# Attention scores of two heads side by side on half the array's rows each, in a hybrid SSD and attention layer

## The chip, the cores and the metric

The kernel runs on one core of a Trainium2 chip. The metric is device time in microseconds (us) of one execution; lower is better. Engines are named as the profile names them: PE is TensorE's matrix product, PEld its loading of weights (the stationary operand), DVE is VectorE, ACT ScalarE, POOL GpSimd, and SP the engine whose queue issues most DMAs. A q behind a name (SPq) is that engine's sequencer.

## What is computed

One decoder layer over 512 tokens of width 1024, all in float32. A normalised input goes through one wide projection; its columns feed a Mamba-2 scan (16 heads) and, beside it, forgetting attention (FoX, 16 heads of 64). Both results go through one output projection, and a gated MLP follows. The part that the change touches is the attention:

```python
qh = rms_norm(heads(q), q_norm_w)
kh = rms_norm(heads(k), k_norm_w)
log_f = jax.nn.log_sigmoid(f_raw + f_bias)
cum = jnp.cumsum(log_f, axis=1).transpose(0, 2, 1)
for start in range(0, s, Q_BLOCK):          # blocks of 128 queries
    end = start + Q_BLOCK
    logits = jnp.einsum('bhqd,bhkd->bhqk', qh[:, :, start:end], kh[:, :, :end]) * HEAD_DIM ** -0.5
    logits = logits + cum[:, :, start:end, None] - cum[:, :, None, :end]
    p = jax.nn.softmax(jnp.where(causal, logits, -jnp.inf), axis=-1)
    outs.append(jnp.einsum('bhqk,bhkd->bhqd', p, vh[:, :, :end]))
```

## The kernel before

Nearly all products are made in a split form. A float32 matrix is written as a high part h, rounded to the fast format float32r, and a low part l, the rest; a product a x b is then the sum of ah x bh, ah x bl and al x bh, three matmuls into one PSUM bank (`mm3`, L97 to L102, so most matmuls of the profile carry line L100). ACT makes h by a copy, DVE makes l by a subtraction, for each weight tile that SP's queue has loaded (`load_split`, L86).

The program is written as a sequence of stages, and a scheduler interleaves them. Parts inside `urgent()` go ahead of the rest when their inputs are ready, and the rest fills up. `tc.keep_in_program_order` pins an instruction: pinned instructions keep the order in which they are written, and others may still be put between them. What stands on an engine in the end is one fixed order, in which each instruction waits for its own inputs.

Stages: at the start (L194 to L219) the transposed input comes in eight tiles, each scaled by the norm's weights into xh and xl (`split_x`, L169), with dt's small product (L205, L209: 64 and 32 columns of the array) and the first wide product (`first_product`, L184) between. Then come projections and the SSD scan, the attention, the second norm, and the MLP ("up" products, and "X", "Y", "Z" for the down-projection).

The attention (L709 to L722) works on pairs of heads, p = 0 to 7:

- `fox_qk` (L545): PE transposes the pair's k and q (tile qkT, L552). The pair's two heads then stand in rows 0 to 63 and 64 to 127 of a PSUM bank. Each head's half is split by ACT (L559) and DVE (L560). For a head, qs holds qh in one half of the rows and ql in the other; ks[.,0] holds kh in both halves and ks[.,1] holds kl in both. The second copy of k is made by ACT and DVE for pair 0 (L562, L563) and by a DMA between partitions for the others (L567).
- `fox_bias` (L570): the forgetting term and the causal mask of a head, written into its tile prob by ACT and POOL.
- `fox_scores` (L592): for each of the four query blocks, with n = 128, 256, 384, 512 keys, two matmuls over all 128 rows (L600, L601) give (qh + ql) x kh + (qh + ql) x kl in one bank, S. DVE then adds the bias and finds the maximum (L602), ACT makes the exponential (L606), and DVE divides (L610).
- `fox_turn` (L612): PE transposes the probabilities (pT, L623), ACT copies them out (L625).
- `fox_values` (L628): PE multiplies by v (o, L633), in plain float32. The two heads of a pair use columns 64 to 127 and 0 to 63 of the array in turn, all pinned. In plain float32 one product is two matmuls in the profile.

The fillers between these steps are projections of later heads (`project`, banks pw; `project_v`, banks pq) and output projections (banks po), all of `mm3`. Banks qkT, S, pT come from one pool of four PSUM banks (`mbank`); pw, pq, po from another of three.

Of the kernel before, what the change touches and what calls it, by code (L numbers as in the profile page):

```python
# [15 lines left out]
P = 128  # L16
# [18 lines left out]
LOW_PART = {}  # L35
C_MIX, C_SCW, C_SCB, C_FCW, C_FCB, C_QW, C_KW, C_END = 0, 8, 56, 68, 200, 244, 245, 246
# [3 lines left out]
def tile_hybrid_layer(  # L40
# [35 lines left out]
    taken = {}  # L76

    def low_part(key):
        order = LOW_PART.get(key, "d")
        n = taken.get(key, 0)  # L80
        taken[key] = n + 1
        return dve if order[n % len(order)] == "d" else pool

    loads = [0]

    def load_split(src, sub=None, four=True):  # L86
# [7 lines left out]
        (sub or dve).tensor_tensor(out=l, in0=r, in1=raw(h), op=ALU.subtract)  # L94
        return h, l
# [73 lines left out]
    def split_x(k, xr):  # L169
        w = pc[:, C_MIX + k : C_MIX + k + 1]  # L170
        act.activation(xh[:, k, :], xr, AF.Copy, scale=w)
# [24 lines left out]
    load_dt()  # L196
    for k in range(NK):
        xr = load_x(k)
        if k == 0:
            nc.sync.dma_start(pc[:, 0:NK], pcol[:, 0:NK])  # L200
        split_x(k, xr)
        if k in (1, 3):
            split_first(*load_first(k // 2))
# [15 lines left out]
    nc.sync.dma_start(pc[:, NK:], pcol[:, NK:])  # L219
# [6 lines left out]
    def feature_tile(src, o=None):  # L226
        h, l = src if isinstance(src, tuple) else load_split(src, sub=low_part("feat"))
# [8 lines left out]
    second, third = [load_split(wxbc[j], sub=dve) for j in (10, 0)]  # L236
# [11 lines left out]
    def out_proj(pairs, m, halves=(0, 1)):  # L248
        for half in halves:
            ws = [load_split(wout[pair, half], sub=low_part("o%d" % pairs[0])) for pair in pairs]  # L250
# [80 lines left out]
    def token_block(src, key="tb"):  # L331
        tiles = [bank("pq") for _ in range(2)]
        for kh in range(2):
            h, l = load_split(src[kh], sub=low_part(key))
# [12 lines left out]

    def wide_block(src, key, use, behind=None):
        ws = []
        for b in range(2):  # L350
            tiles = [bank("pw") for _ in range(2)]
            for kq in range(4):
                if b == 0:
                    ws.append(load_split(src[kq], sub=low_part(key)))
# [190 lines left out]
    def fox_qk(pair, tq, tk):  # L545
        qs = [pf.tile([P, SEQ], F32R, tag="qs", name="qs", bufs=4) for _ in range(2)]
        ks = [pf.tile([P, 2, SEQ], F32R, tag="ks", name="ks", bufs=4) for _ in range(2)]
        pr = pair % 2
        for tok, w in ((tk, kw), (tq, qw8)):
# [3 lines left out]
            for hd, (own, other) in enumerate(HALVES):  # L553
                src, sw = t[own, :], w[own]
                if tok is tq:
                    h, l = qs[hd][own, :], qs[hd][other, :]
                else:
                    h, l = ks[hd][own, 0, :], ks[hd][own, 1, :]
                act.activation(h, src, AF.Copy, scale=sw)  # L559
                dve.scalar_tensor_tensor(out=l, in0=src, scalar=sw, in1=raw(h), op0=ALU.mult, op1=ALU.subtract)  # L560
                if tok is tk and pair == 0:
                    act.activation(ks[hd][other, 0, :], src, AF.Copy, scale=sw)  # L562
                    dve.scalar_tensor_tensor(  # L563
                        out=ks[hd][other, 1, :], in0=src, scalar=sw, in1=raw(h), op0=ALU.mult, op1=ALU.subtract
                    )
                elif tok is tk:
                    nc.sync.dma_start(raw(ks[hd][other, :, :]), raw(ks[hd][own, :, :]))  # L567
        return qs, ks
# [23 lines left out]
    def fox_scores(qs, ks, prob):  # L592
        nm = pf.tile([P, NTB], F32, tag="nm", name="nm", bufs=2)
        sm = pf.tile([P, NTB], F32, tag="sm", name="sm", bufs=2)
        for qb in range(NTB):
            n = (qb + 1) * P
            p = prob[:, QOFF[qb] : QOFF[qb] + n]
            sps = mbank("S")
            qst = qs[:, qb * P : (qb + 1) * P]
            pe.matmul(sps[:, :n], qst, ks[:, 0, :n], start=True, stop=False)  # L600
            pe.matmul(sps[:, :n], qst, ks[:, 1, :n], start=False, stop=True)  # L601
            dve.tensor_tensor_reduce(  # L602
                out=p, in0=sps[:, :n], in1=p, scale=-1.0, scalar=-NEG, op0=ALU.add, op1=ALU.min,
                accum_out=nm[:, qb : qb + 1],
            )
            act.activation(p, p, AF.Exp, scale=-1.0, bias=nm[:, qb : qb + 1], accum_out=sm[:, qb : qb + 1])  # L606
        dve.reciprocal(sm, sm)
        for qb in range(NTB):
            p = prob[:, QOFF[qb] : QOFF[qb] + (qb + 1) * P]
            dve.tensor_scalar(out=p, in0=p, scalar1=sm[:, qb : qb + 1], scalar2=None, op0=ALU.mult)  # L610
# [62 lines left out]
    def start_pair(p):  # L673
        with urgent():
            pairs[p] = fox_qk(p, *qk[p // 2])

    def start_head(n):
        qs, ks = pairs[n // 2]
        with urgent():
            probs[n] = fox_bias(n)  # L680
            fox_scores(qs[n % 2], ks[n % 2], probs[n])
# [28 lines left out]
    start_head(0)  # L710
    start_head(1)
    for n in range(16):
# [7 lines left out]
        if n + 2 < 16:  # L720
            start_head(n + 2)
# [258 lines left out]
def _lay_out(i, np):  # L980
# [6 lines left out]
    def taps(v):  # L987
# [8 lines left out]
            cols(i["norm_mix_w"][0]), taps(i["ssd_conv_w"][0]), cols(i["ssd_conv_b"][0]),  # L996
# [13 lines left out]
        "wdtf": dtf.reshape(8, 128, 32).transpose(1, 0, 2).reshape(128, 256),  # L1010
# [33 lines left out]
```

## Time and profile before

| | |
|---|---|
| median of 3 runs | 800.19 us (799.64 to 801.09) |
| the profiled execution's own time | 800.87 us |
| its span, first to last instruction | 799.1 us |
| PE busy | 792.8 us |
| DVE busy | 568.1 us |
| ACT busy | 427.8 us |
| POOL busy | 213.2 us |
| attention stage, first to last score matmul | 219.1 to 413.9 us |

A row of a timeline reads: start in us, duration in us, engine, line, operation, what it writes <- what it reads, shapes, and how many. A row of a group reads: line, engine, operation, names, shapes, count | busy time in us, mean ns of one | idle time of the engine just before, and what ended it. In names, 128*64 stands for the weights' shape: 128 rows of the array and 64 columns. A row of the windows gives, for a stretch, the busy time of PE, PEld, DVE, ACT and POOL with counts, then the granted clock, the busy share of the DMA engines and GB/s. The chain of work that ended last is followed back from the last instruction, each step to what released it.

### The profile page before, as it was taken

Reading aid. Unit: us, or ns where it says so; the run is one execution under the profiler, and the core shown is the slowest. Engines: PE = TensorE matmul, PEld = TensorE weight load, DVE = VectorE, ACT = ScalarE, POOL = GpSimd, SP = SyncE. Lnnn points to the kernel's source line nnn. Section 1 sums busy time; section 2 is a strip of 40 time slices with the busy share of each in tenths; the row PEclk is TensorE's granted clock in tenths of the full one; section 3 lists DMA queues with packets and bytes.
Section 4 is the critical chain, followed back from the end, with each engine's and each line's share of the span. In section 5 each row is a group of like instructions: output and inputs, shape, how many; then the busy total and the mean of one; then the engine's idle time right before and its main releaser. Section 6 shows DMA issues by size and latency. Waiting matters only on the chain.

```text
span 799.1 us, 10983 instructions
## 1 busy us (share of the span) xinstructions
PE 792.8 (99%) x3981; PEld 656.6 (82%) x3981; DVE 568.1 (71%) x889; ACT 427.8 (54%) x787; POOL 213.2 (27%) x246
## 2 busy tenths in 40 slices
PE   9999999999999999999999999999999999999997
PEld 7888888888989788778977888888888888888886
DVE  4798998688677487667764677766766766778744
ACT  7557646552587695674751563444443444556531
POOL 0003232433225234213101434233333223233120
PEclk9999999999999999999999999999999999999999
DMA  8614331331334243233231363223223223399982
GB/s 326 204 54 143 126 106 62 138 132 52 122 112 137 80 146 113 85 106 104 78 110 54 131 186 106 93 91 107 94 92 105 95 91 105 91 252 193 212 187 93
DMA packets 31398, 98.13 MB, mean 123 GB/s; under 512 B 4016, under 2 KB 5104, under 8 KB 31344
## 3 DMA queue, kind: packets, MB, share of 16 engines
q1 hardware_dynamic: 27456, 85.38, 32.6%
q0 software_dynamic: 3456, 11.54, 8.1%
q8 instruction: 31, 0.51, 0.3%
q10 hardware_dynamic: 432, 0.52, 0.2%
q14 instruction: 23, 0.19, 0.1%
HBM read 91.56 MB, written 2.20 MB: 117 GB/s over the span
## 4 chain that ended last, share of the span: by engine, by line
PE 98%; DMA 1%; ACT 0%; SPq 0%; DVE 0%; DVEq 0%; issue 0%
PE up L100 30%; PE pw L100 17%; PE po L100 11%; PE g L100 7%; PE pq L100 6%; PE Y L100 6%; PE X L100 4%; PE Z L100 4%; PE o L633 2%; PE pT L623 2%; PE yd L462 2%; PE j L100 1%; PE S L601 1%; PE S L600 1%; PE qkT L552 1%; PE yo L468 1%
## 5 line engine op out<-in xcount | busy, mean ns | idle before, releaser
L93 ACT CAST wh<-wraw 128x1024 fp32r<-128x1024 f32 x103 | 107.9, 1050 | 122.7 <-PE up L100 75.5
L94 DVE TENSOR_TENSOR wl<-wraw,wh 128x1024 fp32r<-128x1024 f32 x103 | 132.3, 1287 | 26.2 <-ACT wh L93 22.9
L100 PE MATMUL up<-hh,wh 128*128 128x512 f32 (+1 forms) x360 | 138.9, 386 | 0.0
L100 PE MATMUL up<-hl,wh 128*128 128x512 f32 (+1 forms) x360 | 138.6, 385 | 0.0
L100 PE MATMUL up<-hh,wl 128*128 128x512 f32 (+1 forms) x360 | 138.6, 385 | 0.0
L100 PEld LDWEIGHTS up<-hh,wh 128*128 128x128 f32 x360 | 67.7, 188 | 13.7 <-issue 0.2
L100 PEld LDWEIGHTS up<-hl,wh 128*128 128x128 f32 x360 | 67.7, 188 | 13.5 <-issue 0.2
L100 PEld LDWEIGHTS up<-hh,wl 128*128 128x128 f32 x360 | 67.7, 188 | 13.4
L100 PE MATMUL pw<-wh,xh 128*128 128x512 f32 x192 | 76.8, 404 | 0.0
L100 PE MATMUL pw<-wl,xh 128*128 128x512 f32 x192 | 76.7, 399 | 0.0
L100 PE MATMUL pw<-wh,xl 128*128 128x512 f32 x192 | 75.8, 396 | 0.0
L837 DVE TENSOR_TENSOR up<-up,R 128x512 f32<-128x512 f32 x44 | 30.3, 690 | 58.8 <-PE up L100 58.8
L842 DVE SCALAR_TENSOR_TENSOR ua<-up,pc,ua 128x511 f32<-128x511 f32 (+1 forms) x88 | 66.8, 763 | 1.3
L602 DVE CUSTOM_DVE_ANT_0 prob<-S,prob 128x128 f32<-128x128 f32 (+1 forms) x64 | 30.4, 488 | 36.3 <-PE S L601 36.0
L583 POOL TENSOR_SCALAR prob<-cum,tokS 128x256 f32<-128x256 f32 (+1 forms) x32 | 21.8, 690 | 104.9 <-PE pT L623 96.9
L791 ACT CAST wh<-T 128x1024 fp32r<-128x1024 f32 (+1 forms) x30 | 29.3, 977 | 36.8 <-PE Z L100 15.3
L792 DVE TENSOR_TENSOR wl<-T,wh 128x1024 fp32r<-128x1024 f32 (+1 forms) x30 | 33.7, 1132 | 19.1 <-ACT wh L791 18.8
L606 ACT ACTIVATE prob<-prob,nm 128x128 f32<-128x128 f32 (+1 forms) x64 | 35.8, 561 | 16.7 <-DVE nm L602 15.9
L267 DVE TENSOR_TENSOR x<-po,x 128x512 f32<-128x512 f32 x48 | 32.5, 686 | 14.7 <-PE po L100 14.2
L100 PEld LDWEIGHTS pw<-wh,xl 128*128 128x128 f32 x192 | 36.1, 188 | 7.4 <-issue 0.2
L100 PEld LDWEIGHTS pw<-wl,xh 128*128 128x128 f32 x192 | 36.2, 189 | 7.1 <-issue 0.7
L100 PEld LDWEIGHTS pw<-wh,xh 128*128 128x128 f32 x192 | 36.1, 188 | 7.2 <-issue 0.5
(236 smaller groups left out, 1858.0 us busy)
## 6 DMA issues: line engine op xcount, KB each, us to landing
wraw<-in_wup_dram SPq DMA_DIRECT2D x44, 512.0 KB, 3.3
T<-in_wdown_dram POOLq DMA_DIRECT2D x20, 512.0 KB, 7.4
wraw<-in_wqk_dram SPq DMA_DIRECT2D x16, 512.0 KB, 3.4
wraw<-in_wout_dram SPq DMA_DIRECT2D x16, 512.0 KB, 3.3
wraw<-in_wxbc_dram SPq DMA_DIRECT2D x11, 512.0 KB, 6.2
wraw<-in_wdown_dram SPq DMA_DIRECT2D x10, 512.0 KB, 3.6
T<-in_wdown_dram SPq DMA_DIRECT2D x10, 512.0 KB, 5.8
wraw<-in_wz_dram SPq DMA_DIRECT2D x8, 512.0 KB, 3.3
```

Of the source, the lines that this page charges most:

```text
L93: act.copy(h, r)
L94: (sub or dve).tensor_tensor(out=l, in0=r, in1=raw(h), op=ALU.subtract)
L100: ins = pe.matmul(o, a, b, start=start and n == 0, stop=stop and n == 2, **kw)
L267: dve.tensor_add(dst, banks[tb], dst)
L462: pe.matmul(yd[:, h * HD : (h + 1) * HD], sc[:, h, :], xdt[:, h * HD : (h + 1) * HD], start=True, stop=True)
L583: pool.tensor_scalar(out=b, in0=cum[:, :n], scalar1=-1.0, scalar2=edge, op0=ALU.mult, op1=ALU.add)
L602: dve.tensor_tensor_reduce(out=p, in0=sps[:, :n], in1=p, scale=-1.0, scalar=-NEG, op0=ALU.add, op1=ALU.min, accum_out=nm[:, qb : qb + 1],)
L606: act.activation(p, p, AF.Exp, scale=-1.0, bias=nm[:, qb : qb + 1], accum_out=sm[:, qb : qb + 1])
L791: act.copy(h[:, :n], src[:, :n])
L792: dve.tensor_tensor(out=l[:, :n], in0=src[:, :n], in1=raw(h[:, :n]), op=ALU.subtract)
L837: dve.tensor_mul(xp, o, R2)
L842: dve.scalar_tensor_tensor(out=a[:, s:], in0=xp[:, : SEQ - s], scalar=pc[:, cw + 2 - s : cw + 3 - s], in1=a[:, s:], op0=ALU.mult, op1=ALU.add,
```

## The change

- `fox_qk` splits k and q for both heads at once: one ACT and one DVE operation over 128 partitions each, into tiles h and l. Nothing is copied to the other half of the rows any more, and the DMAs of L567 are gone.
- `fox_scores` takes a pair. For each query block there are three passes (qh x kh, qh x kl, ql x kh), and in each pass a matmul of the first head over rows 0 to 63 and one of the second head over rows 64 to 127, into two banks. Query block 3 and then blocks 0 and 2 make the first pinned block (18 matmuls, four banks), query block 1 the second (6 matmuls, two banks). The first matmul of a block isn't pinned.
- `start_pair` makes the biases of both heads; `score_pair` for the next pair stands between the two turns of this pair.
- The norm weights (8 columns) come in front of dt's weights in one load, and the load of 128x8 in the start is gone.
- `LOW_PART`, which chose an engine for the low parts, is removed; its table was empty, so that the engine stays DVE.

```diff
     def load_dt():
-        w = px.tile([P, NK, 32], F32, tag="wdr", name="wdr")
-        nc.sync.dma_start(w.rearrange("p k m -> p (k m)"), wdtf)
+        raw_dt = px.tile([P, NK + NK * 32], F32, tag="wdr", name="wdr")
+        nc.sync.dma_start(raw_dt, wdtf)
+        w = raw_dt[:, NK:].rearrange("p (k m) -> p k m", m=32)
...
+        return raw_dt[:, 0:NK]
...
-    load_dt()
+    mix = load_dt()
     for k in range(NK):
         xr = load_x(k)
-        if k == 0:
-            nc.sync.dma_start(pc[:, 0:NK], pcol[:, 0:NK])
         split_x(k, xr)
...
     def fox_qk(pair, tq, tk):
...
-        for tok, w in ((tk, kw), (tq, qw8)):
+        split = []
+        for tag, tok, w in (("k", tk, kw), ("q", tq, qw8)):
             t = mbank("qkT")
             for tb in range(NTB):
                 pe.transpose(t[:, tb * P : (tb + 1) * P], tok[:, tb, pr * P : (pr + 1) * P], ident)
-            for hd, (own, other) in enumerate(HALVES):
...
-                    nc.sync.dma_start(raw(ks[hd][other, :, :]), raw(ks[hd][own, :, :]))
+            h, l = [pf.tile([P, SEQ], F32R, tag=tag + x, name=tag + x, bufs=2) for x in "hl"]
+            act.activation(h, t, AF.Copy, scale=w)
+            dve.scalar_tensor_tensor(out=l, in0=t, scalar=w, in1=raw(h), op0=ALU.mult, op1=ALU.subtract)
+            split.append((h, l))
...
+    def fox_scores(q, k, both):
+        nm, sm = [[pf.tile([P, NTB], F32, tag=t, name=t, bufs=4) for _ in range(2)] for t in ("nm", "sm")]
+        for block in (((3,), (0, 2)), ((1,),)):
+            ready = []
+            for qbs in block:
+                banks = [mbank("S") for _ in range(2)]
+                w = 0
+                for qb in qbs:
+                    n = (qb + 1) * P
+                    for step, (a, c) in enumerate(((0, 0), (0, 1), (1, 0))):
+                        for o, rows in zip(banks, HALVES[0]):
+                            ins = pe.matmul(
+                                o[:, w : w + n], q[a][rows, qb * P : (qb + 1) * P], k[c][rows, :n],
+                                start=step == 0, stop=step == 2, skip_group_check=True,
+                            )
+                            if ready or step or o is banks[1]:
+                                tc.keep_in_program_order(ins)
+                    ready.append((qb, [o[:, w : w + n] for o in banks]))
+                    w += n
...
-    start_head(0)
-    start_head(1)
+    score_pair(0)
     for n in range(16):
...
-        if n + 2 < 16:
-            start_head(n + 2)
+        if n % 2 == 0 and n < 14:
+            score_pair(n // 2 + 1)
```

How the instructions stand now shows at three places. On PE, in the first pair's scores, before the change (S is a score matmul, pw a filler):

```order
L100 MATMUL pw<-wh,xh 128x512
L100 MATMUL pw<-wl,xh 128x512
L600 MATMUL S<-ks,qs 128x512
L601 MATMUL S<-ks,qs 128x512
L600 MATMUL S<-ks,qs 128x128
L100 MATMUL pw<-wh,xl 128x512
L100 MATMUL pw<-wh,xh 128x512
L100 MATMUL pw<-wl,xh 128x512
L601 MATMUL S<-ks,qs 128x128
L600 MATMUL S<-ks,qs 128x256
L601 MATMUL S<-ks,qs 128x256
```

And after it, the first pinned block of the same pair (kh and kl, qh and ql are the split tiles; an x2 row is the first and the second head in turn):

```order
L582 MATMUL S<-kh,qh 128x512
L91 MATMUL pw<-wh,xl 128x512
L582 MATMUL S<-kh,qh 128x512
L582 MATMUL S<-kl,qh 128x512 x2
L582 MATMUL S<-kh,ql 128x512 x2
L582 MATMUL S<-kh,qh 128x128 x2
L582 MATMUL S<-kl,qh 128x128 x2
L582 MATMUL S<-kh,ql 128x128 x2
L582 MATMUL S<-kh,qh 128x384 x2
L582 MATMUL S<-kl,qh 128x384 x2
L582 MATMUL S<-kh,ql 128x384 x2
```

The scores, strewn singly and in twos among fillers before, now stand together, except that a filler has come between the first matmul, of the first head, and its counterpart of the second. On PE, at the end of this pair's scores, before the change:

```order
L100 MATMUL pw<-wh,xh 128x512
L100 MATMUL pw<-wl,xh 128x512
L600 MATMUL S<-ks,qs 128x512
L601 MATMUL S<-ks,qs 128x512
L100 MATMUL pw<-wh,xl 128x512
L552 MATMUL qkT<-ident,tok 128x128 x8
L100 MATMUL pw<-wh,xh 128x512
L100 MATMUL pw<-wl,xh 128x512
```

And after it, the second pinned block (query block 1):

```order
L582 MATMUL S<-kh,qh 128x256
L91 MATMUL pw<-wl,xh 128x512
L91 MATMUL pw<-wh,xl 128x512
L91 MATMUL pw<-wh,xh 128x512
L582 MATMUL S<-kh,qh 128x256
L582 MATMUL S<-kl,qh 128x256 x2
L582 MATMUL S<-kh,ql 128x256 x2
L542 MATMUL qkT<-ident,tok 128x128 x8
```

Here three fillers stand between the two heads of the first pass. Over the whole program S stands in 54 unbroken stretches before and 28 after; of the 28, nine are one matmul of the first head alone, and the two heads of a pass stand apart in 14 of 96 cases (three of 512 columns, five of 256, six of 128). On SP, the first DMA issues, before the change:

```order
L178 DMA wdr<-in_wdtf_dram 128x256
L156 DMA xr<-in_xT_dram 128x512
L200 DMA pc<-in_pcol_dram 128x8
L156 DMA xr<-in_xT_dram 128x512
L162 DMA wr<-in_wxbc_dram 128x512
L156 DMA xr<-in_xT_dram 128x512 x2
```

And after it:

```order
L169 DMA wdr<-in_wdtf_dram 128x264
L147 DMA xr<-in_xT_dram 128x512 x2
L153 DMA wr<-in_wxbc_dram 128x512
L147 DMA xr<-in_xT_dram 128x512 x2
L153 DMA wr<-in_wxbc_dram 128x512
```

The small load of pc has gone, and every later load stands one place further ahead.

More of the change, by code (lines that the diff above doesn't have):

```diff
@@ L34 @@
 WARM = 8
[L35 to L36 removed]
+C_SCW, C_SCB, C_FCW, C_FCB, C_QW, C_KW, C_END = 0, 48, 60, 192, 236, 237, 238
 @with_exitstack
@@ L74, in raw, with load_split @@
         return ap.bitcast(F32)
[L76 to L82, printed above, removed]
     loads = [0]
-    def load_split(src, sub=None, four=True):
+    def load_split(src, four=True):
         r = wp.tile([P, 1024], F32, tag="wraw", name="wraw", bufs=3)
@@ L234, in feature_tile @@
         return o
-    second, third = [load_split(wxbc[j], sub=dve) for j in (10, 0)]
+    second, third = [load_split(wxbc[j]) for j in (10, 0)]
     for tb in range(NTB):
@@ L249, in out_proj @@
         for half in halves:
-            ws = [load_split(wout[pair, half], sub=low_part("o%d" % pairs[0])) for pair in pairs]
+            ws = [load_split(wout[pair, half]) for pair in pairs]
             banks = {}
@@ L333, in token_block @@
         for kh in range(2):
-            h, l = load_split(src[kh], sub=low_part(key))
+            h, l = load_split(src[kh])
             for b in range(2):
@@ L552, in fox_qk @@
                 pe.transpose(t[:, tb * P : (tb + 1) * P], tok[:, tb, pr * P : (pr + 1) * P], ident)
-            for hd, (own, other) in enumerate(HALVES):
[L554 to L568, printed above, removed]
+            h, l = [pf.tile([P, SEQ], F32R, tag=tag + x, name=tag + x, bufs=2) for x in "hl"]
+            act.activation(h, t, AF.Copy, scale=w)
+            dve.scalar_tensor_tensor(out=l, in0=t, scalar=w, in1=raw(h), op0=ALU.mult, op1=ALU.subtract)
+            split.append((h, l))
+        return split[1], split[0]
     def fox_bias(head):
```

61 lines of the change are left out of this document (29 added, 32 removed).

## The prediction

> **What bounds the kernel now.** I read the page first, then the chain of work that ended last, then the waits of TensorE alone.
>
> ```profile
> span 799.1 us, 10983 instructions
> PE 792.8 (99%) x3981; PEld 656.6 (82%) x3981; DVE 568.1 (71%) x889; ACT 427.8 (54%) x787; POOL 213.2 (27%) x246
> PE 98%; DMA 1%; ACT 0%; SPq 0%; DVE 0%; DVEq 0%; issue 0%
> by line: PE up L100 30.0%; PE pw L100 16.7%; PE po L100 11.2%; PE g L100 7.0%; PE pq L100 5.8%; PE Y L100 5.6%; PE X L100 3.8%; PE Z L100 3.7%; PE o L633 2.3%; PE pT L623 2.2%; PE yd L462 1.7%; PE j L100 1.4%; PE S L601 1.3%; PE S L600 1.3%
> PE g L195 <- DVE mhalf L120: 1.0, 1, 1.0
> PE g L205 <- ACT xh L171: 0.3, 1, 0.3
> ```
>
> The first two rows are of the page, then the chain by engine and by line, then all of TensorE's waits (total, times, longest). TensorE carries 98% of the chain and waits for nobody after the first microseconds. So this change is worth what it adds to or takes from TensorE's own stream, plus what it does in the first 8 us, where data are not there yet. The scores, S, hold 1.3% + 1.3% of 799.1 us: **20.8 us**.
>
> A busy matmul's duration (0.39 us) isn't its price, since matmuls overlap; the price is the step from one start to the next. The timeline of TensorE in the attention stage gives it (start, duration):
>
> ```profile
> 219.06 0.22 PE L600 MATMUL S<-ks,qs 128*128 128x128 f32 x1
> 219.12 0.45 PE L100 MATMUL pw<-wh,xl 128*128 128x512 f32 x1
> 219.41 0.28 PE L600 MATMUL S<-ks,qs 128*128 128x256 f32 x1
> 219.53 0.39 PE L100 MATMUL pw<-wh,xh 128*128 128x512 f32 x1
> 222.52 0.33 PE L600 MATMUL S<-ks,qs 128*128 128x384 f32 x1
> 222.70 0.34 PE L601 MATMUL S<-ks,qs 128*128 128x384 f32 x1
> 224.71 0.39 PE L600 MATMUL S<-ks,qs 128*128 128x512 f32 x1
> 224.94 0.39 PE L601 MATMUL S<-ks,qs 128*128 128x512 f32 x1
> ```
>
> A step is 0.23 us at 512 columns, about 0.17 at 384 (0.18 here), 0.12 at 256. At 128 it is 0.06, but the next matmul then holds 0.29 in place of 0.23: its weights weren't there yet. So a 128-wide matmul costs 0.06 to 0.12, and I take 0.11. Of the same stage comes a look at the value products, o, which work on two halves of the array:
>
> ```profile
> 277.64 0.39 PE L100 MATMUL pw<-wh,xh 128*128 128x512 f32 x1
> 277.87 0.40 PE L600 MATMUL S<-ks,qs 128*128 128x512 f32 x1
> 278.20 2.38 PE L633 MATMUL o<-pt,v 128*64 128x512 f32 x16
> 280.50 0.51 PE L601 MATMUL S<-ks,qs 128*128 128x512 f32 x1
> 280.85 0.60 PE L552 MATMUL qkT<-ident,tok 128*128 128x128 f32 x4
> 91.84 0.86 PE st L475 x2
> ```
>
> The last row is of the chain: a plain-float32 product is two matmuls, and over 512 columns each takes 0.43 us. The 16 of o (two heads, four key blocks, two matmuls each) stream 2 x 2 x 1,280 = 5,120 columns: one after the other 5,120/512 x 0.43 = 4.3 us. They took 2.30. So the heads on the two column halves run at the same time, 2.15 us of streaming. What they cost beside that: 0.33 - 0.23 = 0.10 us before the first, 2.30 - 2.15 = 0.15 within, and 0.35 - 0.23 = 0.12 after (the 512-wide S holds 0.35). **One stay in the split array costs 0.37 us for going in and out.**
>
> **The change part by part.**
>
> *Scores, streaming.* Before, each head needs two passes over 1,280 columns with all 128 rows, four for a pair. After, three passes of each head over 64 rows. If the heads overlap as o's do, a pair takes three: 3 x (0.23 + 0.17 + 0.12 + 0.11) = 1.89 us, times 8 = 15.1 us. But the written order keeps the two heads of a pass apart in 14 places (three 512 wide, five 256, six 128), where other matmuls stand between them; there each streams alone: 3 x 0.23 + 5 x 0.12 + 6 x 0.11 = 1.95 us more. Sum 17.1 us against 20.8: **-3.7 us**.
>
> *Going in and out.* This has no row of its own: no matmul of before uses half the rows. In the order of the changed kernel S stands in 28 unbroken stretches; 9 are one lone matmul of the first head (rows 0 to 63), 19 hold both heads. The nearest rows lie at two ends. o pays 0.37 us. The other end is the start of the kernel, where dt's products use 64 and 32 columns of the array between full ones:
>
> ```profile
> 9.67 0.40 PE L100 MATMUL g<-xh,wl 128*128 128x512 f32 x1
> 9.90 0.39 PE L205 MATMUL g<-xh,wdt 128*64 128x512 f32 x1
> 10.14 0.40 PE L100 MATMUL g<-xh,wh 128*128 128x512 f32 x1
> 10.37 0.39 PE L209 MATMUL g<-xl,wdt 128*32 128x512 f32 x1
> 10.60 0.39 PE L100 MATMUL g<-xl,wh 128*128 128x512 f32 x1
> ```
>
> All steps are 0.23 or 0.24: a narrower shape that starts at the array's first column costs nothing. What o has and dt lacks is a product that does not begin at the array's origin and runs beside another. The 19 stretches with both heads have that too, in rows; the 9 lone ones begin at row 0 and are like dt. So I take 19 x 0.37 = **+7.0 us**. Ends: 0 and 28 x 0.37 = 10.4. It could reach below nothing only if S's own entry were cheaper than a full matmul's, which is already free, so no gain is in it.
>
> *Start.* The 128x8 load of the norm weights goes, and they come with dt's weights. DMA issues, the first activations that scale x, and the first wide product:
>
> ```profile
> 1.17 0.42 SPq L156 DMA_DIRECT2D xr<-in_xT_dram  x1
> 1.65 0.42 SPq L200 DMA_DIRECT2D pc<-in_pcol_dram  x1
> 2.11 0.43 SPq L156 DMA_DIRECT2D xr<-in_xT_dram  x1
> 4.10 0.72 ACT L171 ACTIVATE xh<-xr,pc 128x512 fp32r<-128x512 f32 x1 [0.80 <-DMA pc<-in_pcol_dram]
> 6.71 0.72 ACT L171 ACTIVATE xh<-xr,pc 128x512 fp32r<-128x512 f32 x1 [1.89 <-DMA xr<-in_xT_dram]
> 8.02 0.50 PE L100 MATMUL g<-xh,wh 128*128 128x512 f32 x1
> 3.00:5.00 2.00, 1.86 (x10) 1.59 (x10) 0.15 (x1) 1.02 (x2) 0.97 (x2) 1.00 1.02 286
> ```
>
> Every later issue moves up by one place, 2.11 - 1.65 = 0.46 us. The first xh no longer waits for pc, but that wait isn't the one that counts: the chain goes through the second x (6.71). That load was issued at 2.11 and landed 4.6 us later, while the DMA engines were full (the last row is a stretch of the windows: DMA share 1.02). A full queue hands on only part of an earlier issue. Bounds 0 and -0.46; I take the middle, **-0.25 us**.
>
> *Off the path.* Splitting q and k:
>
> ```profile
> L559 ACT ACTIVATE qs<-qkT,qw 64x512 fp32r<-64x512 f32 x16 | 11.0, 685 | 1.7 <-DVE qs L560 1.6
> L560 DVE SCALAR_TENSOR_TENSOR qs<-qkT,qw,qs 64x512 fp32r<-64x512 f32 x16 | 12.0, 750 | 1.7 <-ACT qs L559 1.3
> L567 SPq DMA_DIRECT2D ks<-ks x14: 461/467/527, 232.9 to 398.9; - x14
> ```
>
> Half of these go (q shown; k is alike): two operations on 128 partitions for a pair and side instead of four on 64, some 11 us of ACT and 12 of DVE, and 14 copies of k between partitions, each 0.47 us of SP's queue. Price 0: TensorE waited for none of them, and the projections and out-projections, which stand between the steps of a pair, cover them. What is late next is the prob work of a pair, which TensorE doesn't wait for either. Moving both heads' biases ahead is Pool and ACT work under the same cover, 0.
>
> *Banks.* A pinned block of 18 matmuls writes four banks, all of its pool; once begun, TensorE can't pass it, and the projections behind it wait too. Its banks come free by copies of transposed probabilities:
>
> ```profile
> L625 ACT COPY pt<-pT 128x512 f32<-128x512 f32 (+1 forms) x48 | 23.3, 513 | 6.1 <-PE pT L623 5.8
> ```
>
> One such copy, 0.51 us, late once in each of 8 blocks would be +4.1 us. In the order the block mostly begins after ten and more other matmuls (2.3 us and up) behind the last transposes, so I take 0.
>
> *Sum:* -3.7 + 7.0 - 0.25 = **+3.0 us**. The profiled execution took 800.87 us, of which 799.1 are the span; the median of the runs shown is 800.19, 0.7 below. The work removed and added is the same in both, so I put the sum on the median: **803.2 us**. With a toll of 0.25 to 0.45 us a stay (4.8 to 8.6) and the start's bounds, this case alone spans 800.8 to 805.1.
>
> **The rivals.**
>
> 1. *Half rows switch for free* (other side). In rows nothing has to be led to another column, and the dt rows show that a smaller shape alone is free; against it speaks o, which pays each time. Place: L582, the 19 stretches. 800.19 - 3.7 - 0.25 = 796.2 us. It decides below (3.7 + 0.25)/19 = 0.21 us a stay. Chance 0.32.
> 2. *Every change of shape empties the array*, lone matmuls too: 28 x 0.37 = 10.4, so 800.19 - 3.7 + 10.4 - 0.25 = 806.6 us. o speaks for it, the dt rows against it, since they change shape at full pace. Chance 0.09. The Trainium skill, "TensorEngine Tiling (Array Packing)", section "Tiling Modes", has this rule: a change of tiling mode, not just of tile, drains the engine. By that rule it would be 806.6 us; o's 0.37 us agrees with it, dt's 0.23 us steps do not.
> 3. *Only one side of the stay costs*, 0.19 us: 19 x 0.19 = 3.6, so 799.8 us, no change. Chance 0.11.
> 4. *The heads do not overlap fully*: two weight loads in turn, 0.11 each, make every pair at least 0.23 us: 24 x 4 x 0.23 + 1.95 = 24.0, +3.2 in place of -3.7, so 810.1 us. o's halves load side by side, but half as wide. Chance 0.04.
> 5. *The blocks wait for banks* on top of my case: 803.2 + 4.1 = 807.3 us. Chance 0.04.
>
> The change does what it says in the written order, apart from the 14 broken pairs, which are in the sum.
>
> **How the numbers follow.** Forecast 0.40, rivals 0.32, 0.09, 0.11, 0.04, 0.04. About 0.2% (1.6 us) is what a measurement of this kernel can tell from no change, so "same" is 798.6 to 801.8. Faster: rival 1 and a quarter of rival 3, 0.35. Same: the rest of rival 3 and a tenth of my own case, 0.12. Slower: what is left, 0.53. The range must reach to rival 1 with its start at the full 0.46 and some cheaper pairs (795.6), and up to the top of my case (805.2); rivals 2, 4 and 5 stay outside, 0.17.
>
> **What would show it.** In the timeline of the changed kernel the two heads' S should start within some 10 ns of each other; S in the chain should fall to about 17 us plus its tolls; the step into a stretch should be about 0.1 us long, the matmul behind it should hold some 0.12 too much, and a lone S should be followed at the plain pace. Steps without these extras mean rival 1. Extras around lone ones mean rival 2. A start of the second head one full step after the first means rival 4. TensorE waiting on ACT or DVE ahead of S means rival 5. The first wide product should start at about 7.8 us rather than 8.02. The forecast is wrong if a stay costs under 0.21 us.

## The result, and the profile after

The changed kernel takes **807.22 us** (median of 4 runs, 806.81 to 807.6) against 800.62 of the kernel before beside it (4 runs, 799.64 to 801.09). The ratio is 1.0081, with a 95% interval of 1.0069 to 1.0093. It is slower, as forecast, but by 6.6 us and not by 3.0, and 807.22 lies above the range's end of 805.2. The profiled execution took 806.81 us, 805.0 of them the span.

The first row is of the page, then the chain by line (the view ends where the row does), then all of TensorE's waits (total, times, longest), each for the changed kernel:

```profile
PE 799.3 (99%) x4045; PEld 653.3 (81%) x4045; DVE 552.7 (69%) x871; ACT 416.0 (52%) x769; POOL 215.9 (27%) x246
```

```profile
by line: PE up L91 29.8%; PE pw L91 16.8%; PE po L91 11.3%; PE g L91 6.9%; PE pq L91 5.9%; PE Y L91 5.6%; PE X L91 3.7%; PE Z L91 3.7%; PE S L582 2.7%; PE o L628 2.3%; PE pT L618 2.3%; PE yd L453 1.7%; PE j L91 1.4%; PE qkT L542 0.9%; PE yo
```

```profile
PE g L188 <- DVE mhalf L111: 1.0, 1, 1.0
```

TensorE still bounds the kernel, and the view shows no wait after the first microseconds: no bank was late. DVE lost 15.4 us of work and ACT 11.8, about what the prediction counted, and neither moved the end. S holds 2.7% of 805.0 us, 21.7, where 17.1 and tolls were forecast; but about half of a toll falls on the matmuls beside a stretch, which the chain puts down to pw, po, pq and pT. The timeline of TensorE (start, duration) shows where it falls:

```profile
219.47 0.39 PE L91 MATMUL pw<-wh,xh 128*128 128x512 f32 x1
219.71 0.39 PE L91 MATMUL pw<-wl,xh 128*128 128x512 f32 x1
220.03 0.50 PE L582 MATMUL S<-kh,qh 64*128 64x512 f32 x1
220.45 0.49 PE L91 MATMUL pw<-wh,xl 128*128 128x512 f32 x1
220.88 0.50 PE L582 MATMUL S<-kh,qh 64*128 64x512 f32 x1
220.88 0.73 PE L582 MATMUL S<-kl,qh 64*128 64x512 f32 x2
221.22 0.62 PE L582 MATMUL S<-kh,ql 64*128 64x512 f32 x2
221.46 0.22 PE L582 MATMUL S<-kh,qh 64*128 64x128 f32 x1
...
222.36 0.33 PE L582 MATMUL S<-kh,ql 64*128 64x384 f32 x1
222.62 0.50 PE L91 MATMUL pw<-wh,xh 128*128 128x512 f32 x1
```

Between two plain pw a step is 0.23 or 0.24 us. The step onto the lone S at 220.03 is 0.32, the S itself holds TensorE for 0.42, and the pw behind it, which stands before the next stretch as well, for 0.43: 0.09 + 0.19 + 0.11 = **0.39 us for one lone product** of the first head. The other eight lone ones hold much the same. The stretch at 220.88 goes in and out the same way. Within it products of the two heads start together (220.88 twice), and the next size begins at 221.46: five products of 512 columns in 0.58 us, where one after the other would take 1.15. They overlap as forecast.

Summed from each start to the next, with the extra time of the matmuls on either side (what they hold beyond their plain step, counted once where a matmul stands between two stretches), S took 27.8 us in 28 stretches, against 21.3 in the kernel before. Such sums, here and below, hang on what is taken as the plain step, by 0.1 to 0.2 us. That is +6.5 us, and the whole attention stage lost 7.1: TensorE was 1.26 us ahead at its 100th pw and 5.87 behind at hT, the transposes that come after the attention.

At the start, a row of ACT, and then one of TensorE:

```profile
3.93 1.40 ACT L162 ACTIVATE xh<-xr,wdr 128x512 fp32r<-128x512 f32 x2 [0.57 <-DMA xr<-in_xT_dram]
```

```profile
7.32 0.39 PE L91 MATMUL g<-xh,wh 128*128 128x512 f32 x1
```

The first two xh run one behind the other from 3.93 on, while in the kernel before the second began at 6.71, after a wait of 1.89 for its data. The first wide product starts at 7.32, 0.70 us ahead of before's 8.02, and TensorE is 1.20 us ahead when the first rbc product begins (26.57 against 27.78; rbc spreads the norm's factors over the rows and comes after the first wide products).

### The profile page after: what moved, and what is told of

It reads as the page before. It is cut to its first block, busy times and chain, and to the rows that moved or that the text cites. A ratio compares the mean times of both kernels' runs of the same rounds, so it can differ in the third digit from the quotient of the medians.

```text
span 805.0 us, 11001 instructions
## 1 busy us (share of the span) xinstructions
PE 799.3 (99%) x4045; PEld 653.3 (81%) x4045; DVE 552.7 (69%) x871; ACT 416.0 (52%) x769; POOL 215.9 (27%) x246
## 4 chain that ended last, share of the span: by engine, by line
PE 99%; DVE 0%; DVEq 0%; issue 0%
PE up L91 30%; PE pw L91 17%; PE po L91 11%; PE g L91 7%; PE pq L91 6%; PE Y L91 6%; PE X L91 4%; PE Z L91 4%; PE S L582 3%; PE o L628 2%; PE pT L618 2%; PE yd L453 2%; PE j L91 1%; PE qkT L542 1%; PE yo L459 1%; PE st L466 1%
## 5 line engine op out<-in xcount | busy, mean ns | idle before, releaser
L562 POOL TENSOR_SCALAR prob<-cum,tokS 128x256 f32<-128x256 f32 (+1 forms) x32 | 22.8, 721 | 106.8 <-PE pT L618 101.6
L258 DVE TENSOR_TENSOR x<-po,x 128x512 f32<-128x512 f32 x48 | 32.7, 688 | 25.9 <-PE po L91 25.6
L785 ACT CAST wh<-T 128x1024 fp32r<-128x1024 f32 (+1 forms) x30 | 29.3, 976 | 36.9 <-PE Z L91 15.3
L598 ACT ACTIVATE prob<-prob,nm 128x128 f32<-128x128 f32 (+2 forms) x64 | 35.5, 556 | 16.1 <-DVE nm L594 15.8
L594 DVE CUSTOM_DVE_ANT_0 prob<-S,prob 128x128 f32<-128x128 f32 (+2 forms) x64 | 27.8, 487 | 17.1 <-PE S L582 16.2
```

What stands on the lines that cost most here:

```text
L258: dve.tensor_add(dst, banks[tb], dst)
L562: pool.tensor_scalar(out=b, in0=cum[:, :n], scalar1=-1.0, scalar2=edge, op0=ALU.mult, op1=ALU.add)
L594: dve.tensor_tensor_reduce(out=p, in0=parts[i], in1=p, scale=-1.0, scalar=-NEG, op0=ALU.add, op1=ALU.min, accum_out=nm[i][:, qb : qb + 1],)
L598: act.activation(p, p, AF.Exp, scale=-1.0, bias=nm[i][:, qb : qb + 1], accum_out=sm[i][:, qb : qb + 1])
L785: act.copy(h[:, :n], src[:, :n])
```

## The experiments

Theory 1: each change between the whole array and half of its rows costs, so an unbroken stretch of S costs about 0.4 us, one lone product like a block of 18. Its rivals put the loss down to the start, to late banks, or to the stretches' surroundings instead of the rows. The first four kernels had the kernel before beside them at 800.57 us (15 runs).

**Start alone.** The kernel before, with the norm weights loaded in front of dt's:

```
-        w = pc[:, C_MIX + k : C_MIX + k + 1]
+        w = mix[:, k : k + 1]
...
-    load_dt()
+    mix = load_dt()
...
-            nc.sync.dma_start(pc[:, 0:NK], pcol[:, 0:NK])
```

> The kernel before with the start of the changed one alone: the norm weights come with dt's weights, and the 128x8 load is gone; scores as before. If the start's gain seen in the trace of the changed kernel (its TensorE runs 1.2 us ahead of the old one from the first wide products to the end of the first projections) belongs to this edit and is carried to the end: 800.6 - 1.2 = 799.4 us, first wide product at about 7.3 us. If that lead was chance of the one execution, or my term was right: 800.4 us, first wide product at 7.8 or later.

801.46 us, ratio 1.0014 (1.0002 to 1.0025). TensorE's waits:

```profile
PE S L600 <- DMA ks<-ks: 1.4, 1, 1.4
PE g L197 <- DVE mhalf L120: 1.0, 1, 1.0
PE g L100 <- ACT wh L166: 0.6, 1, 0.6
```

TensorE is 0.57 us ahead at the first rbc product and loses it: in the order that the scheduler now writes, one S comes before the copy of k that it needs has landed, 1.4 us. Both expected times, 799.4 and 800.4 us, were missed. By itself the start brings nothing, and it explains none of the loss.

**Whole blocks, opened by pinned writes.** A small VectorE write into every bank of a block, kept in program order, holds the block's first product until all banks are free, so that 16 whole stretches are left (in each pass the second head now comes first):

```
+            held = [mbank("S") for _ in range(2 * len(block))]
+            for t in held:
+                tc.keep_in_program_order(dve.memset(t[:, 0:1], 0.0))
...
-                            if ready or step or o is banks[1]:
+                            if not first:
                                 tc.keep_in_program_order(ins)
```

> The changed kernel with the score blocks made whole: a one-column memset by DVE of each bank ahead of the block lets its first matmul start only when all its banks are free, so S stands in 16 stretches (18 and 6 matmuls) instead of 28, and no head streams alone. Theory 1 (every stretch of 64-row matmuls pays about 0.40 us, lone ones too, and inside it the heads overlap): S is 15.1 + 16 x 0.40 = 21.5 us, some 6.0 less than in the changed kernel: about 801 us, within 1 us of the kernel before. Theory 2 (only stretches with both heads pay, the rest of the loss lies elsewhere): 807.2 - 1.95 - 3 x 0.37 = 804.1 us. Theory 3 (TensorE waits for banks at the pinned blocks): the gates make that no better, 807 us or more.

803.81 us, ratio 1.0041 (1.0027 to 1.0055); S 21.7 us. S is what theory 1 said. The whole is not: by itself the time would fit theory 2's 804.1. But o, whose products lay in 8 stretches, lies in 13, and takes 22.5 us with its neighbours, not 20.1; with S's 0.4 that is 2.8 of the 3.2 us above the kernel before.

**Four blocks of six, opened in the same way.** More stretches, 33:

```
-        for block in (((3,), (0, 2)), ((1,),)):
+        for block in (((3,),), ((0,),), ((2,),), ((1,),)):
```

> As gated_blocks, but each query block is a block of its own: S stands in 33 stretches, nearly all of six matmuls with both heads; the same matmuls, the same streaming. Theory 1: 17 stretches more than gated_blocks at 0.40 each, +6.8 us, so about 807.5 us. Theory 2: the same step per stretch, but from 804.1: 810 us. Theory 3: fewer banks are held at once, so it should be faster than gated_blocks.

816.39 us, ratio 1.0192 (1.0178 to 1.0206); S 30.2 us, of which 1.5 are waits; o in 15 stretches, 24.7 us. All three expectations (807.5, 810, faster) were missed. Waits of TensorE appear as well; of eight, this one is for an opening write:

```profile
PE S L587 <- DVE S L577: 0.7, 1, 0.7
```

L577 writes into a bank of S that TensorE then waits for. The direction is right, but the kernel's time says little about the toll.

**One block of all 24, in six banks, opened in the same way,** the two heads interleaved so that each has a product under way, 8 stretches:

```
+            shared = po.tile([P, 512], F32, tag="o", name="S")
+            held = [mbank("S") for _ in range(4)]
+            spare = bank("S")
+            for t in [shared, spare] + held:
+                tc.keep_in_program_order(dve.memset(t[:, 0:1], 0.0))
...
+            while todo[0] or todo[1]:
+                i = 0 if not todo[1] or (todo[0] and spent[0] <= spent[1]) else 1
```

> As gated_blocks, but one stretch of 24 matmuls per pair, 8 in all: the second block's two banks come from the pool of o and the pool of the fillers, and the two heads' matmuls are interleaved so that both rows stay busy. Theory 1: S is 15.1 + 8 x 0.40 = 18.3 us against 21.3 before and about 27.5 in the changed kernel: about 797.5 us, faster than both, provided that the borrowed banks hold nothing up. Theory 2: 801.1 us. Theory 3: slower than gated_blocks, since six banks must be free at once.

815.25 us, ratio 1.018 (1.0165 to 1.0194), though S fell to 18.45 us. TensorE's waits, then a stretch of the windows with the second of them (length, busy PE, PEld, DVE, ACT, POOL, granted clock, DMA share, GB/s):

```profile
PE qkT L542 <- DVE tok L519: 4.9, 1, 4.9
PE o L639 <- ACT pt L631: 4.7, 1, 4.7
```

```profile
240.00:248.00 8.00, 3.28 (x20) 2.60 (x18) 6.71 (x26) 7.91 (x22) 1.86 (x4) 0.86 0.30 102
248.00:252.90 4.90, 4.53 (x16) 1.71 (x16) 1.58 (x4) 1.65 (x4) 3.31 (x3) 0.53 0.50 161
```

Two waits of almost 5 us, and behind this one the clock was granted at 0.53, so that 4.9 us held 16 matmuls. The gain on S was real and was lost elsewhere. The outcome is theory 3's, slower than the whole blocks; whether the six banks or the pinned writes did it, this kernel doesn't tell.

**The changed kernel with full rows.** The same instructions in the same order on every engine, only the rows differ:

```
-                                o[:, w : w + n], q[a][rows, qb * P : (qb + 1) * P], k[c][rows, :n],
+                                o[:, w : w + n], q[a][:, qb * P : (qb + 1) * P], k[c][:, :n],
```

> The changed kernel with every score product over all 128 rows instead of its head's 64: the same instructions in the same order on every engine, the same banks, waits and 28 stretches; only the rows differ (both heads of a pair then get the same, summed scores, so this leaves the right scores out). The two heads' products can no longer overlap, so the 192 products stream one after another: 48 sets of four sizes at the 0.648 us that a set took in the kernel before (20.73 us / 32) are 31.1 us, with their neighbours some 31.7 us against 28.0 in the changed kernel. Theory 1 (the 0.40 us per stretch are the price of going into and out of 64 rows): no toll is left, a first product of a stretch steps 0.23 us like the next, the product behind a stretch steps 0.23 too, TensorE's time on S is 31 to 32 us and the kernel takes 810 to 812 us. Rival (the 0.40 us belong to the stretches whatever the rows: to the new banks, the first write of a bank, or operands that come late): the toll stays, S is 42 to 43 us and the kernel takes 820 to 823 us.

810.35 us, ratio 1.0113 (1.0099 to 1.0127), beside 801.24 of the kernel before (15 runs), which stood beside the next three too. The same place of TensorE's timeline:

```profile
219.76 0.39 PE L91 MATMUL pw<-wl,xh 128*128 128x512 f32 x1
219.99 0.39 PE L582 MATMUL S<-kh,qh 128*128 128x512 f32 x1
220.22 0.40 PE L91 MATMUL pw<-wh,xl 128*128 128x512 f32 x1
220.45 0.39 PE L582 MATMUL S<-kh,qh 128*128 128x512 f32 x1
220.68 0.62 PE L582 MATMUL S<-kl,qh 128*128 128x512 f32 x2
```

Every step is 0.23 us, and S takes 30.8 us, a little under the 31 to 32 expected: nothing but streaming without overlap. The toll belongs to the half rows; banks, order and tiles are the same, and without half rows they cost nothing. The rival is out.

**The scores alone.** The changed kernel with before's start (the reverse of the first diff); in the order that follows, S lies in 33 stretches.

> The change without its start: the norm weights come in their own load again, as in the kernel before; the scores, q and k are the changed kernel's. In the order as written the scores then lie in 33 stretches instead of 28. Theory 1 (0.40 us per stretch, lone ones too): S about 30.0 us (28.0 and 5 x 0.40) against 21.3 in the kernel before, so 809 to 810.5 us, and the start worth about 1 us to the changed kernel's median. Rival (the start term was right at 0.25 us, and a lone stretch costs nothing): the paired stretches alone pay, and the kernel takes 806.5 to 808 us.

809.85 us, ratio 1.0108 (1.0092 to 1.0124); S 30.1 us. Five stretches more than in the changed kernel, three of them lone, cost 2.3 us of S, and the ratios differ by 0.0027, 2.2 us. That is theory 1's side. What the start is worth can't be told from two ratios of this width.

**Whole blocks, opened by writes that are free to move.** As the second kernel, but the writes aren't pinned; only the block's first product waits for them; 18 stretches:

```
+            gates = [dve.memset(t[:, 0:1], 0.0) for t in held]
...
+                            if first:
+                                for gate in gates:
+                                    tc.add_manual_dep(
+                                        ins.ins, gate.ins.name,
+                                        mybir.DependencyInfo(mybir.DependencyClass.Sync, mybir.DependencyReason.DATA), reason="banks",
+                                    )
```

> The changed kernel with each block of scores whole, in 18 stretches instead of 28: the first product of a block waits for small writes into all the banks that the block uses, and these writes are free to take any place in VectorE's order instead of a pinned one. Theory 1 (0.41 us per stretch, and what the pinned writes cost earlier was VectorE's work held behind them): S about 22.5 us (15.1 and 18 x 0.41), o, pT and po as in the kernel before within 1 us each, 800 to 802 us. Rival (a block that waits for its four banks costs waits by itself, whoever opens them): o, pT and po stay 1.5 us or more above the kernel before, 803 us or more.

806.92 us, ratio 1.0069 (1.0057 to 1.0082). S is 22.3 us as theory 1 had it, but the other half of that expectation fell: the time didn't improve over pinned writes, it got worse. The rival's 803 us or more came, but not the waits that it named: TensorE has only 1.8 us of them, all in the first microseconds of the kernel. o is what differs: 16 stretches and 24.4 us (the 25.5 of a later expectation counts a transpose between two stretches twice, as does the 22.8 for the next kernel). So neither theory named the cause; the next kernel shows it.

**One block of 24, opened by writes that are free to move.**

```
-            for t in [shared, spare] + held:
-                tc.keep_in_program_order(dve.memset(t[:, 0:1], 0.0))
+            gates = [dve.memset(t[:, 0:1], 0.0) for t in [shared, spare] + held]
...
```

> All 24 score products of a pair in one stretch, 8 stretches in all, in six banks whose opening writes are free to take any place in VectorE's order; the earlier form with pinned opening writes took 815.25 us with S at 18.45 us. Theory 1 (0.41 us per stretch, the rest was VectorE's work held behind the pinned writes): S about 18.4 us, 2.9 below the kernel before, and with the start's 0.5 to 1.2 us 796 to 798 us if no new wait appears. Rival (six banks at once are too many: whoever opens them, transposes and o products wait for the banks' readers): S is 18.4 us all the same, but TensorE shows waits of several us before or behind the stretches, and the kernel takes 805 us or more.

801.35 us, ratio 0.9999 (0.999 to 1.0007): the two long waits are gone, and with them and the half clock behind them 14 us; the six banks are the same, so it was the pinned writes that made them. S is 18.45 us, 2.9 under the kernel before, yet the time is the same, between the two expectations. TensorE's timeline at the third pair's o:

```profile
306.98 1.72 PE L644 MATMUL o<-pt,v 128*64 128x512 f32 x6
308.62 0.33 PE L634 MATMUL pT<-ident,prob 128*128 128x128 f32 x1
308.88 0.86 PE L644 MATMUL o<-pt,v 128*64 128x384 f32 x2
309.67 0.33 PE L634 MATMUL pT<-ident,prob 128*128 128x128 f32 x1
309.94 0.65 PE L644 MATMUL o<-pt,v 128*64 128x256 f32 x2
...
311.61 0.44 PE L644 MATMUL o<-pt,v 128*64 128x128 f32 x4
311.98 0.51 PE L91 MATMUL po<-wh,mfh 128*128 128x512 f32 x1
```

The 16 matmuls of o are no longer one stretch: four transposes of another head stand between them, and from 306.98 to the next po at 311.98 pass 5.0 us where a whole stretch holds TensorE for 2.3. Each transpose ends a stretch on o's half columns and begins another, and between two of them stands a single product of one head (384 wide, 0.79 us), so that the two heads don't overlap there. In all o has 12 stretches and 22.1 us here, 2.0 more than in the kernel before. S and o together would still leave the kernel 0.9 us faster; why it isn't stays open.

**Both, with o whole.** In the two kernels above, each transpose is queued behind the last o product written before it:

```
                     ins = pe.transpose(t[:, w : w + P], prob[:, o : o + P], ident)
+                    if last:
+                        tc.add_manual_dep(
+                            ins.ins, last[-1].ins.name,
+                            mybir.DependencyInfo(mybir.DependencyClass.NoSync, mybir.DependencyReason.DATA), reason="behind o",
+                        )
...
+        last.append(ins)
```

The form with blocks:

> The form with whole blocks of 18 and 6 (19 stretches of S in this order), and every pair's o products whole, in 8 stretches instead of the 16 that this form had. Theory 1: S about 22.7 us (22.3 and one stretch more), o 20.0 instead of 25.5 us, so 806.9 - 5.5 + 0.4 = 801.8, 801 to 802.5 us. Rival (o's broken stretches were a sign of banks that came late, and the wait shows elsewhere once o is whole): 804 us or more with waits of TensorE on ScalarE or VectorE at o or pT.

802.37 us, ratio 1.0016 (1.0007 to 1.0025), beside 800.74 (23 runs): in the expected 801 to 802.5; S 22.8, o 19.8 us in 8 stretches. The ratio fell by 0.0053, 4.2 us, about o's 4.6 less S's 0.5. The form with one block:

> The form with all 24 score products of a pair in one stretch, 8 stretches, and beside it every pair's o products whole again: a transpose of a later head may no longer be issued between them, so that o lies in 8 stretches as in the kernel before, not in 12. Theory 1 (every change between whole and split array pays, o's as S's): S stays at 18.4 us, o goes back from 22.8 to 20.0 us with its neighbours, and the kernel takes 798 to 799 us, 0.2 to 0.35% below the kernel before: the first form faster than both. Rival (what held the earlier form at the time of the kernel before is not o's stretches but the six banks, taken together so early that other work is late): o's sum falls but waits or slow stretches take it back, 800.5 to 802 us.

**799.87 us, ratio 0.9986 (0.9977 to 0.9994).** This is the one form faster than both kernels, by 0.14% of the kernel before, less than theory 1's 0.2 to 0.35% and better than its rival's 800.5. TensorE's timeline at a stretch of S, and its waits:

```profile
222.36 0.40 PE L91 MATMUL pw<-wh,xh 128*128 128x512 f32 x1
222.69 0.49 PE L592 MATMUL S<-kh,qh 64*128 64x512 f32 x2
...
224.54 0.34 PE L592 MATMUL S<-kh,ql 64*128 64x384 f32 x2
224.81 0.50 PE L91 MATMUL pw<-wl,xh 128*128 128x512 f32 x1
225.15 0.40 PE L91 MATMUL pw<-wh,xl 128*128 128x512 f32 x1
```

```profile
PE g L188 <- DVE mhalf L111: 1.0, 1, 1.0
PE po L91 <- ACT mfh L660: 0.7, 1, 0.7
PE g L91 <- ACT wh L157: 0.5, 1, 0.5
PE po L91 <- DVE x L258: 0.3, 1, 0.3
```

All 24 products of a pair are through in 2.12 us, with one step in (0.33) and one out (0.34). S is 18.4 us. Against the form before it the ratio fell by 0.0013, 1.0 us, and o by 1.5, from 22.1 to 20.6. What is missing to the expectation is partly seen: o could fall by no more than that, since a po waits 0.7 us for o's copy, with 0.3 more at L258, and TensorE was 0.4 us ahead at the 100th pw, not 1.2. S and o together are 2.4 us below the kernel before, the kernel 1.1; the rest isn't assigned.

**dt with half the rows.** The prediction took dt's rows as the price of a lone product. This is the kernel before with dt's 16 products over the first 64 rows, and so with half of dt's sum left out; the order is the same:

```
-        ins = pe.matmul(pdt[:64, :], wdt[:, k, :], xh[:, k, :], start=k == 0, stop=False, skip_group_check=True)
+        ins = pe.matmul(pdt[:64, :], wdt[0:64, k, :], xh[0:64, k, :], start=k == 0, stop=False, skip_group_check=True)
...
-            pdt[:32, :], wdt[:, k, 0:32], xl[:, k, :], start=False, stop=k == NK - 1, skip_group_check=True
+            pdt[:32, :], wdt[0:64, k, 0:32], xl[0:64, k, :], start=False, stop=k == NK - 1, skip_group_check=True
```

> The kernel before, with dt's 16 products over the first 64 of their 128 rows (half of dt's sum is left out); the same instructions in the same order on every engine. Each of these products lies alone between full ones, and from 8.6 us on, for 13 of them, TensorE waits for nothing. In the kernel before they use 64 or 32 columns and all rows, and step 0.23 us. Theory 1 (half the rows is what pays, a lone product at the array's origin included; fewer columns at the origin are free): each pays some 0.09 us before it, 0.20 in its own step and 0.11 behind it, as the lone score products of the changed kernel do; 13 x 0.40 = 5.2 us more at the first rbc, and 805 to 807 us in all. Rival (a lone narrow product beginning at the origin is free, as the forecast took it from dt's rows, and the lone score products paid for their neighbourhood: new banks, a high priority, operands just written): steps stay 0.23 us, 800 to 801.5 us.

815.69 us, ratio 1.0191 (1.0174 to 1.0208), beside 800.64 (7 runs). TensorE's timeline in the profiled execution, then its windows, and under them one of the kernel before:

```profile
14.78 0.69 PE L205 MATMUL g<-xh,wdt 64*64 64x512 f32 x1
15.39 0.79 PE L100 MATMUL g<-xh,wh 128*128 128x512 f32 x1
16.12 0.63 PE L209 MATMUL g<-xl,wdt 64*32 64x512 f32 x1
16.68 0.79 PE L100 MATMUL g<-xl,wh 128*128 128x512 f32 x1
17.27 0.63 PE L100 MATMUL g<-xh,wl 128*128 128x512 f32 x1
17.83 0.69 PE L205 MATMUL g<-xh,wdt 64*64 64x512 f32 x1
...
30.34 0.63 PE L100 MATMUL g<-xl,wh 128*128 128x512 f32 x1
30.77 0.63 PE L100 MATMUL g<-xh,wl 128*128 128x512 f32 x1
```

```profile
12.00:18.00 6.00, 6.00 (x11) 2.17 (x10) 4.13 (x7) 4.51 (x7) 0.00 (x0) 0.50 1.03 417
24.00:30.00 6.00, 6.00 (x12) 2.53 (x12) 0.54 (x2) 0.28 (x1) 0.00 (x0) 0.50 0.29 92
30.00:36.00 6.00, 6.00 (x25) 4.89 (x24) 1.23 (x1) 0.77 (x1) 0.00 (x0) 0.88 0.27 90
```

```profile
12.00:18.00 6.00, 6.00 (x27) 4.36 (x26) 4.05 (x7) 4.53 (x6) 0.00 (x0) 1.00 1.03 419
```

The rival is out: the same products, alone and at the array's origin, pay as soon as they use half the rows. The size was expected at 5.2 us and is 13.8 (the first rbc product begins at 41.57, not 27.78), and in this execution the clock stayed at 0.50 until 31 us. The five matmuls from 14.78 to 17.83 take 3.05 us; at this clock a plain step is 0.43 (30.34 to 30.77), five are 2.13, and the 0.92 left over are 0.46 for each of the two narrow ones. In the kernel before, five steps took 1.17. So of 1.88 us more in a round, half is the toll and half the clock. That holds for the profiled execution. The four took 814.72, 815.16, 816.31 and 816.23 us, and the mean granted clock was 0.985 in the first two, which fits 24 us at 0.50, but 0.999 in the last two: these lost as much without such a stretch on record, and no trace shows how.

## Why the prediction was wrong

**What bounds the kernel: right.** TensorE alone sets the end in both kernels; what left ACT, DVE and SP's queue was worth nothing.

**Streaming, -3.7 us: right.** The heads overlap. The forms with whole stretches lie on a line, 18.44 us of S at 8 stretches and 22.76 at 19: (22.76 - 18.44)/11 = 0.39 us a stretch, and 18.44 - 8 x 0.39 = 15.3 us are left for streaming, where 15.1 were forecast. With the 1.95 us for the broken pairs the changed kernel should then have 15.3 + 1.95 + 28 x 0.39 = 28.2 us of S; it has 27.8. Rival 4, no overlap, is out.

**Going in and out: the step that failed.** The price of a stretch was right, 0.37 from o against 0.39 measured; that was in part luck, since o's price is of half columns and no row of before used half the rows. The number of stretches that pay was wrong: the prediction took "the 9 lone ones begin at row 0 and are like dt", 19 x 0.37 = 7.0 us, where all 28 pay, 28 x 0.39 = 10.9. The 3.9 us between the two are about what lies between 803.2 and 807.22. The prediction's own sign for it, extras around lone products, is in the timeline above. dt's products are narrower in columns and use every row; they were nearest in standing alone, and not in shape. Full rows in S (no toll) and half rows in dt (toll) turn the question round from both sides, and each time the rows decide. So it is rival 2 that held, with its 806.6 us, though not as it was worded: not every change of shape pays, since dt's 64 and 32 columns at the origin step 0.23 us. The Trainium skill, "TensorEngine Tiling (Array Packing)", section "Tiling Modes", has the rule that a change of tiling mode drains TensorE; the lone S rows agree at 0.39 us. dt's 64 and 32 columns at the origin, at steps of 0.23 us, agree only if they are no change of mode, which no run shows.

**Start, -0.25 us: small either way.** In the profile it was 1.2 us, beyond the bound of 0.46. But at the 100th pw the ten profiled executions with this start are 0.3 to 1.3 us ahead of before's, and the scores alone, with the old start, are 0.4 ahead too; and by itself the start brought no time. The prediction read the late second x, 1.89 us of wait, as the rule; it was partly chance of that execution. With the old start the second xh waited 1.89, 1.19 (dt with half the rows) and not at all (the scores alone), with the new one 0 to 0.35 us. That the load's place in the queue is gone is seen; its size stays open between nothing and about 1 us.

**Off the path and banks, 0: right in the changed kernel.** The trace shows not one wait of TensorE on banks or prob work, so rival 5 is out too; rivals 1 and 3, half rows free or paid on one side only, fell with the 0.39 us. Where pinned opening writes took that cover away, two waits of 4.9 and 4.7 us appeared in one kernel; the same six banks opened by free writes had none of them.

**What remains.** Of the 7.1 us that the attention stage lost, S and its neighbours hold 6.5; 0.6 is not assigned.

## What to carry to other kernels

Count the unbroken stretches that use part of the array's rows in the order as it is issued, lone products included, and put a price on each (0.4 us here) before you count what the overlap saves: here 28 stretches ate three times the gain, and 8 made it a gain. Look for the nearest row by what the array does (rows or columns, origin or not), not by where the instruction stands. And when one group is made whole, check whether the scheduler has broken up another: o's broken stretches took back 2.0 of the 2.9 us that S had won.

## What the runs showed of the hardware that was not expected

In one execution, lone half-row products went with a clock that stayed at half. With dt's 16 products on half the rows, TensorE shows as busy 6.00 of 6.00 us in each stretch of the windows from 12 to 30 us, and the granted clock is 0.50 all that time; the last narrow product began at 28.33, the full step of 0.23 us came at 31.55. The kernel before, with the same order, had 1.00 from 6 us on. Whether the changes of shape or the fewer rows at work kept it down isn't told apart, and two of the four executions lost as much time at a mean granted clock of 0.999, so that the clock can't be called the cause of their loss. The Trainium skill, "TensorE: Matmul & The Clock Gate", "Part 1: The HAM clock gate (the "warmup" mystery)", has the clock rise after a window of about 3.4 us of sustained work. The trace of the profiled execution agrees only if part of what shows as busy isn't work in this sense, which no run here shows by itself. Later in the kernel, with the clock up and longer work between them, the 28 stretches of the changed kernel left it at 1.00.
